# Product-key experts in another order: every query before the first batch of expert rows

## The chip, the cores and the metric

The kernel runs on one core of a Trainium2 chip. The metric is the device time of one execution in microseconds (us); the lower it is, the better.

## The reference, cut to what matters

A token sequence of 256 rows of 1024 numbers goes through two blocks: a mixer and the PEER layer, then a second mixer and a mixture of 16 dense experts. The change is in the PEER layer:

```python
q = (hf @ wq).reshape(T, PEER_HEADS, 2, PEER_QDIM // 2)          # T 256, 8 heads, 2 x 128
s = jnp.einsum('thpd,hpnd->thpn', q, subkeys)                    # 128 keys in each half
s1, i1 = lax.top_k(s[:, :, 0], 16); s2, i2 = lax.top_k(s[:, :, 1], 16)
...                                                              # 256 sums, the best 16 of them
w = jax.nn.softmax(top_s, axis=-1)                               # idx: 16 of 16384 experts
act = gelu(einsum('cd,chkd->chk', x_c, u[idx_c]))
out = einsum('chk,chkd->cd', w_c * act, v[idx_c])
```

So each token picks 8 x 16 = 128 experts, and each expert is one row of u and one row of v, 1024 float32 numbers each.

## The kernel before

The program is written as one fixed order of instructions for each engine. Four stages follow one another: `mixer1`, `peer`, `mixer2` and `experts`. The 128 partitions hold 128 tokens; there are two token tiles `tt`.

**Memory.** `Mem` hands out columns of one tile of 42440 floats per partition: `take` gives the lowest hole that is large enough, `give` returns a region. A region handed out again must wait for the readers and writers of its former content.

**Weights.** `Stream` brings the weight blocks of the first three stages in their order: 19 blocks `w_in`, 8 of `w_branch` and `w_out`, 8 blocks `wq`, then those of the second mixer, `w_in_2`. Each block is 1 MB, 2048 floats per partition, and lands in a landing region by a DMA on SP's queue. Each half of a block is then split (`split`, lines 277 and 281) into a high part (a copy on ACT) and a low part (a subtraction on DVE, or on POOL where the half's number modulo 4 is in `on_pool`). There are three landing regions and three part buffers, so the split runs three halves ahead of TensorE. When both halves of a block are split, its landing region is free: `ahead` loads the next block into it, or gives it back where `shrink` asked for that. `done` frees a part buffer and calls `ahead`, and so the next split stands in the program right behind the use of a half.

**PEER before.** Head `c` needs block `wq + c`: `features` runs 24 matmuls for each half (line 266), ACT copies the query to `qT`, and `score(c)` multiplies it by the keys (8 matmuls, two copies on ACT, line 986). `search` is a generator of DVE work for 16 pairs of token tile and head; it finds the best 16 of 128 twice (lines 971 to 974), the best 16 of 256 sums and their indices (lines 999 to 1022). `look(us)` puts about so many planned microseconds of this search on DVE; it does nothing where the scores of the next head are not there. A *slot* is one chosen expert of each of the 128 tokens of a tile; there are 256. `gather` issues for each slot an indirect DMA from POOL (line 1049) that brings 128 rows of u and v, 1 MB, into one of `RING = 10` row buffers; it may run 10 slots ahead of the finished batches, and it first puts on DVE whatever search a slot's indices still need. A `batch` handles two slots: two dot products on DVE (line 1065), Gelu on ACT (1067), a `look`, the coefficient on DVE (1069), two diagonal matrices on ACT (1073) and 4 products of 128 x 512 on TensorE, which add the v rows, scaled, into the accumulators. A row buffer is free after its slot's products.

In the loop over the 8 heads of the kernel before, the first ten gathers stand behind head 1, and one batch stands behind each of the heads 5, 6 and 7. After the loop come the other 125 batches, with `close_tile` after each token tile. When the search is over, `preload` takes regions for the second mixer out of the regions that the search leaves.

**Experts.** `Ahead` loads the experts' 192 blocks of 2 MB one after the other into regions of 4096 floats at fixed positions. `ex.take` claims those positions that are wholly free: two early in `mixer2` (line 1273), others at lines 1567 and 1680, the rest in `experts` (line 1732).

Of the kernel before, what the change touches and what calls it, by code (L numbers as in the profile page):

```python
# [14 lines left out]
OP = mybir.AluOpType  # L15
AX = mybir.AxisListType

T, D = 256, 1024
# [4 lines left out]
RING, BATCH = 10, 2  # L23
# [150 lines left out]
class Mem:  # L174
# [5 lines left out]
    def take(self, n, high=False):  # L180
        n = (n + 7) // 8 * 8
        fits = [h for h in self.holes if h[1] >= n]
        assert fits, (n, self.holes)
        h = max(fits) if high else min(fits)
        self.holes.remove(h)
        at = h[0] + h[1] - n if high else h[0]
        rest = (h[0], h[1] - n) if high else (h[0] + n, h[1] - n)
        if rest[1]:
            self.holes.append(rest)
        return at, n  # L190

    def claim(self, at, n):

        for h in self.holes:
            if h[0] <= at and at + n <= h[0] + h[1]:
                self.holes.remove(h)
                self.holes += [x for x in ((h[0], at - h[0]), (at + n, h[0] + h[1] - at - n)) if x[1]]
                return True
        return False
# [16 lines left out]
class Kernel:  # L216
# [17 lines left out]
    def sb(self, n, high=False):  # L234
        r = self.mem.take(n, high)
        return r, self.mem.at(r, n)
# [28 lines left out]
    def mm(self, out, l, r, start=True, stop=True):  # L265
        self.nc.tensor.matmul(out, l, r, start=start, stop=stop, skip_group_check=True)  # L266
# [664 lines left out]
    def peer(self):  # L931
        nc, a, mem = self.nc, self.a, self.mem
        sb, rb, drop = self.scope()
        mm = self.mm
        st, wq = self.st, self.blocks_at["wq"]
        sub = sb(2048, "keys").rearrange("p (c n) -> p c n", c=16)
        nc.scalar.dma_start(sub, a["subkeys"])
        gain = sb(D, "gain")
# [1 line left out]
        h2 = [rb(8 * T, "h2").rearrange("p (k t) -> p k t", k=8) for _ in range(2)]  # L940
        self.scaled(self.h, self.v("nffn"), *h2)
        mem.give(self.junk_region)
        st.on_pool = ()
        st.shrink(land=1)

        xn = sb(2 * D).rearrange("p (t d) -> p t d", t=2)
        for tt in range(2):
            nc.vector.scalar_tensor_tensor(xn[:, tt], self.h[:, tt], self.rs[:, tt:tt + 1], gain,
                                           op0=OP.mult, op1=OP.mult)
        drop("gain")  # L950
        self.preload_norm()
        S = [sb(2048, "scores").rearrange("p (c n) -> p c n", c=16) for _ in range(2)]
        qT = [sb(512, "keys").rearrange("p (c t) -> p c t", c=2) for _ in range(2)]

# [7 lines left out]
        idx, w, act, coef = [[sb(128) for _ in range(2)] for _ in range(4)]  # L962
        total = [sb(8) for _ in range(2)]
        diags = [sb(128) for _ in range(2 * BATCH)]
        ring = [sb(2 * D) for _ in range(RING)]

        def top16(x, v, ix):

# [9 lines left out]
        def score(h):  # L978

            b, ps = self.bank()  # L980
            for tt in range(2):
                for s in range(2):
                    mm(ps[:, (2 * tt + s) * 128:(2 * tt + s) * 128 + 128],
                       qT[h % 2][:, s, tt * 128:tt * 128 + 128], sub[:, 2 * h + s])
            for tt in range(2):
                nc.scalar.copy(S[tt][:, 2 * h:2 * h + 2],
                               ps[:, 256 * tt:256 * tt + 256].rearrange("p (c n) -> p c n", c=2))
            self.free_banks.append(b)
            self.scored = h + 1
# [38 lines left out]
        def look(us):  # L1028

            nonlocal debt  # L1030
            debt += us
            while debt > 0 and (self.searched % 8 < self.scored or self.searched >= 8):
                took = next(todo, 0)
                if not took:
                    break
                debt -= took
            debt = min(debt, 0.0)
# [5 lines left out]
        def gather():  # L1043
            nonlocal gathered
            while gathered < slots and gathered < batches * BATCH + RING:
                n, tt, k = gathered, gathered // 128, gathered % 128
                while self.searched <= n // 16:
                    next(todo)
                nc.gpsimd.indirect_dma_start(  # L1049
                    out=ring[n % RING], out_offset=None, in_=a["peer_uv"],  # L1050
                    in_offset=bass.IndirectOffsetOnAxis(ap=idx[tt].bitcast(U32)[:, k:k + 1], axis=0))
                gathered += 1

        def batch():

            nonlocal batches
            gather()
            first = batches * BATCH
            tt, k0 = divmod(first, 128)
            here = slice(k0, k0 + BATCH)  # L1060
            if k0 == 0:
                acc[2 * tt:2 * tt + 2] = [self.bank() for _ in range(2)]
            for k in range(BATCH):
                x = ring[(first + k) % RING][:, 0:D]
                nc.vector.tensor_tensor_reduce(x, x, xn[:, tt], 1.0, 0.0, OP.mult, OP.add,  # L1065
                                               act[tt][:, k0 + k:k0 + k + 1])
            nc.scalar.activation(act[tt][:, here], act[tt][:, here], AF.Gelu)  # L1067
            look(SEARCH)
            nc.vector.scalar_tensor_tensor(coef[tt][:, here], act[tt][:, here], total[tt][:, k0 // 16:k0 // 16 + 1],  # L1069
                                           w[tt][:, here], op0=OP.mult, op1=OP.mult)  # L1070
            for k in range(BATCH):
                g = diags[(first + k) % len(diags)]
                nc.scalar.activation(g, self.ident, AF.Copy, scale=coef[tt][:, k0 + k:k0 + k + 1])  # L1073
            for k in range(BATCH):
                g, x = diags[(first + k) % len(diags)], ring[(first + k) % RING]
                for n in range(2):
                    mm(acc[2 * tt + n][1], g, x[:, D + n * 512:D + n * 512 + 512], k0 + k == 0, k0 + k == 127)
            batches += 1

        for c in range(8):  # L1080
            b, ps = self.bank()
            for half in range(2):
                self.features(wq + c, h2, ps, (half,))
                look(KEYS)
            nc.scalar.copy(qT[c % 2], ps.rearrange("p (c t) -> p c t", c=2))
            self.free_banks.append(b)
            if c:
                score(c - 1)
            if c == 1:
                gather()  # L1090
            if c > 4:
                batch()
        score(7)
        drop("h2")
        while batches * BATCH < 128:
            batch()
        drop("keys")
# [1020 lines left out]
```

## Time and profile before

| what | value |
|---|---|
| median of 3 runs | 2134.71 us (2130.98 to 2134.91) |
| the profiled execution | 2133.23 us, of which the span of its instructions is 2131.4 us |
| TensorE busy | 1538.2 us, 72% |
| VectorE (DVE) busy | 844.7 us, 40% |
| ScalarE (ACT) busy | 434.8 us, 20% |
| GpSimd (POOL) busy | 372.5 us, 17% |
| moved by DMA | 734.01 MB, mean 344 GB/s |

The profile's times count from the span's start. A busy share is an average over stages with different limits, so the stages are read one by one. In the views, L1049 is line 1049 of the kernel before, PEld is TensorE's weight load, and SPq stands for a DMA issued from SP's queue. The bracket at the end of a timeline line says how long the engine had been idle and what ended that.

### The profile page before, as it was taken

What the parts mean: (1) busy time and instruction counts of PE and PEld (TensorE: products, weight loads), DVE (VectorE), ACT (ScalarE), POOL (GpSimd) and SP (SyncE); (2) the same over time, 40 slices, a digit from 0 to 9 for tenths busy, and PEclk for the clock granted to TensorE, in tenths of its full rate; (3) what the DMA queues carried; (4) which work ended last, traced back from release to release, by engine and by line L of the source; (5) the groups of instructions that cost most, each with busy time, mean ns of one, the idle gap of its engine ahead of it and who ended that gap; (6) DMA issues with size and microseconds to landing.
All of it is one profiled execution on the core that took longest, in us unless ns stands there. A gap on an engine that the chain in (4) does not pass through costs nothing.

```text
span 2131.4 us, 21789 instructions
## 1 busy us (share of the span) xinstructions
PE 1538.2 (72%) x8331; PEld 779.0 (37%) x8331; DVE 844.7 (40%) x1993; ACT 434.8 (20%) x1014; POOL 372.5 (17%) x337
## 2 busy tenths in 40 slices
PE   8999866877777777778899776565555556565656
PEld 7988843323323222227888511111111111111112
DVE  6656758999946555556852400000000000000002
ACT  4554433323312111114432300000000000000002
POOL 1000213444444333324322200000000000000000
PEclk9999978999999999999999887888888887878887
DMA  6333476999999999992123699999999999999997
GB/s 239 139 119 128 159 308 265 421 421 421 421 420 397 421 422 422 421 416 119 62 85 136 254 429 429 427 427 427 428 428 427 428 428 428 428 428 427 426 428 313
DMA packets 74986, 734.01 MB, mean 344 GB/s; under 512 B 8321, under 2 KB 9089, under 8 KB 10114
## 3 DMA queue, kind: packets, MB, share of 16 engines
q1 hardware_dynamic: 37154, 460.29, 51.9%
q0 software_dynamic: 36864, 268.45, 30.5%
q10 hardware_dynamic: 864, 3.87, 0.5%
q8 instruction: 66, 1.08, 0.2%
q14 instruction: 38, 0.31, 0.0%
HBM read 731.53 MB, written 1.05 MB: 344 GB/s over the span
## 4 chain that ended last, share of the span: by engine, by line
issue 47%; PE 19%; DVE 16%; DMA 15%; POOL 1%; ACT 1%; POOLq 0%; SPq 0%; ACTq 0%; DVEq 0%
PE bank L266 18%; DMA sbuf<-in_peer_uv_dram,sbuf 15%; DVE sbuf L1065 6%; DVE sbuf L972 2%; DVE sbuf L971 1%; POOL sbuf L1049 1%; DVE sbuf L974 1%; DVE rounded L281 1%; DVE sbuf L1232 1%; DVE sbuf L1017 0%; DVE sbuf L1018 0%; DMA sbuf<-in_wq_dram 0%; DVE sbuf L1015 0%; ACT rounded L277 0%; PE bank L800 0%
## 5 line engine op out<-in xcount | busy, mean ns | idle before, releaser
L266 PE MATMUL bank<-sbuf 128*32 128x512 f32 (+8 forms) x4032 | 927.8, 576 | 389.9 <-DMA sbuf<-in_wgu_dram 184.3
L266 PEld LDWEIGHTS bank<-sbuf 128*128 128x128 f32 (+5 forms) x3980 | 386.0, 163 | 908.4 <-issue 311.5
L1065 DVE CUSTOM_DVE_ANT_0 sbuf<-sbuf 128x1024 f32<-128x1024 f32 x256 | 308.8, 1223 | 147.8 <-DMA sbuf<-in_peer_uv_dram,sbuf 147.7
L1049 POOL DMA_INDIRECT sbuf<-in_peer_uv_dram,sbuf x256 | 268.1, 1047 | 431.3 <-PE bank L266 252.4
L266 PE MATMUL bank<-rounded 128*128 128x256 f32 (+3 forms) x2208 | 304.1, 298 | 3.6 <-DVE rounded L281 3.3
L266 PEld LDWEIGHTS bank<-rounded 128*128 128x128 f32 (+2 forms) x2208 | 285.1, 193 | 16.6 <-DVE rounded L281 3.7
L1889 DVE TENSOR_TENSOR rest<-rest,bank 128x512 f32<-128x512 f32 x16 | 11.0, 688 | 539.4 <-PE bank L266 539.4
L353 POOL TENSOR_TENSOR sbuf<-sbuf 128x1 f32<-128x1 f32 (+2 forms) x11 | 10.0, 913 | 1177.3 <-DVE sbuf L357 942.7
L266 PE MATMUL bank<-sbuf,tail 128*32 128x512 f32 (+1 forms) x960 | 131.8, 684 | 83.1 <-DMA sbuf<-in_wd_dram 78.6
L281 DVE TENSOR_TENSOR rounded<-sbuf,rounded 128x1024 fp32r<-128x1024 f32 (+2 forms) x90 | 101.7, 1146 | 97.8 <-ACT rounded L277 97.8
L277 ACT CAST rounded<-sbuf 128x1024 fp32r<-128x1024 f32 (+3 forms) x112 | 107.5, 974 | 156.6 <-PE bank L266 128.4
L1888 ACT ACTIVATE rest<-bank 128x512 f32<-128x512 f32 x16 | 9.6, 597 | 567.2 <-PE bank L266 567.2
L1881 DVE TENSOR_SCALAR sbuf<-sbuf 128x256 f32<-128x256 f32 x16 | 6.6, 414 | 292.4 <-PE bank L266 292.4
L1073 ACT ACTIVATE sbuf<-sbuf 128x128 f32<-128x128 f32 x256 | 89.1, 394 | 132.6 <-DVE sbuf L1069 127.1
L266 PE MATMUL bank<-tail,sbuf 128*32 128x512 f32 (+2 forms) x344 | 73.5, 738 | 35.1 <-DMA tail<-in_wgu_dram 23.5
L1067 ACT ACTIVATE sbuf<-sbuf 128x2 f32<-128x2 f32 x128 | 26.0, 204 | 349.3 <-DVE sbuf L1065 349.2
L266 PEld LDWEIGHTS bank<-sbuf,tail 128*32 128x32 f32 x960 | 29.2, 124 | 175.8 <-DMA sbuf<-in_wd_dram 119.0
L1909 ACT COPY tail<-bank 128x512 f32<-128x512 f32 x15 | 8.8, 585 | 292.7 <-PE bank L266 292.7
L281 POOL TENSOR_TENSOR rounded<-sbuf,rounded 128x1024 fp32r<-128x1024 f32 x22 | 53.4, 2433 | 78.4 <-ACT rounded L277 64.6
L266 PEld LDWEIGHTS bank<-tail,sbuf 128*32 128x32 f32 (+2 forms) x344 | 21.9, 164 | 90.1 <-DMA tail<-in_wgu_dram 37.2
L266 PE MATMUL bank<-rest,sbuf 128*32 128x512 f32 (+1 forms) x196 | 33.0, 775 | 22.0 <-DMA rest<-in_wgu_dram 22.0
L1069 DVE SCALAR_TENSOR_TENSOR sbuf<-sbuf 128x2 f32<-128x2 f32 x128 | 27.7, 216 | 23.8 <-ACT sbuf L1067 23.8
(274 smaller groups left out, 852.8 us busy)
## 6 DMA issues: line engine op xcount, KB each, us to landing
sbuf<-in_wgu_dram SPq DMA_DIRECT2D x104, 2048.0 KB, 39.1
sbuf<-in_wd_dram SPq DMA_DIRECT2D x48, 2048.0 KB, 39.1
sbuf<-in_w_in_dram SPq DMA_DIRECT2D x29, 1024.0 KB, 4.9
tail<-in_wgu_dram SPq DMA_DIRECT2D x12, 2048.0 KB, 39.1
rest<-in_wgu_dram SPq DMA_DIRECT2D x12, 2048.0 KB, 39.1
rest<-in_wd_dram SPq DMA_DIRECT2D x6, 2048.0 KB, 39.1
tail<-in_wd_dram SPq DMA_DIRECT2D x6, 2048.0 KB, 39.1
sbuf<-in_w_out_dram SPq DMA_DIRECT2D x8, 1024.0 KB, 4.8
```

What stands on the lines that cost most here:

```text
L266: self.nc.tensor.matmul(out, l, r, start=start, stop=stop, skip_group_check=True)
L277: nc.scalar.copy(hi.bitcast(FR), x)
L281: e.tensor_tensor(lo.bitcast(FR), x, hi, op=OP.subtract)
L971: nc.vector.max(v[:, cut], x)
L972: nc.vector.max_index(ix[:, cut].bitcast(U32), v[:, cut], x)
L974: nc.vector.match_replace(x, v[:, cut], x, -3.0e38)
L1049: nc.gpsimd.indirect_dma_start(out=ring[n % RING], out_offset=None, in_=a["peer_uv"], in_offset=bass.IndirectOffsetOnAxis(ap=idx[tt].bitca ...
L1065: nc.vector.tensor_tensor_reduce(x, x, xn[:, tt], 1.0, 0.0, OP.mult, OP.add, act[tt][:, k0 + k:k0 + k + 1])
L1067: nc.scalar.activation(act[tt][:, here], act[tt][:, here], AF.Gelu)
L1069: nc.vector.scalar_tensor_tensor(coef[tt][:, here], act[tt][:, here], total[tt][:, k0 // 16:k0 // 16 + 1], w[tt][:, here], op0=OP.mult, op ...
L1073: nc.scalar.activation(g, self.ident, AF.Copy, scale=coef[tt][:, k0 + k:k0 + k + 1])
L1232: nc.vector.scalar_tensor_tensor(y[:, i], x[:, i, j:j + 256], w[:, j:j + 1], y[:, i], op0=OP.mult, op1=OP.add)
```

## The change

All eight `wq` blocks get a landing region at once: right after the scaled activations are made, the stream grows by five regions and is told to give six back as they come free. The row buffers of the ring are no longer taken all at once at the start; each of the first ten gathers takes one if a hole of 2048 floats exists, and stops if none does. The loop over heads holds no batch any more. `score(c - 1)` stands between the two halves of head `c`, the first `gather` stands there for head 1, and the heads from 2 on end with a `gather`. The normalised token rows `xn` (`normed`) are made behind the first gathers and no longer before the loop, some low parts go to POOL until then (`on_pool = (0, 2)`), and `preload_norm` (the load of one gain vector, and a region) moves behind the loop.

```diff
+    def fits(self, n):
+        return any(h[1] >= n for h in self.holes)
...
         self.scaled(self.h, self.v("nffn"), *h2)
         mem.give(self.junk_region)
-        st.on_pool = ()
-        st.shrink(land=1)
-
+
+        st.on_pool = (0, 2)
+        st.grow(land=5)
+        st.shrink(land=6)
         xn = sb(2 * D).rearrange("p (t d) -> p t d", t=2)
-        for tt in range(2):
-            nc.vector.scalar_tensor_tensor(xn[:, tt], self.h[:, tt], self.rs[:, tt:tt + 1], gain,
-                                           op0=OP.mult, op1=OP.mult)
-        drop("gain")
-        self.preload_norm()
+
+        def normed():
+
+            for tt in range(2):
+                nc.vector.scalar_tensor_tensor(xn[:, tt], self.h[:, tt], self.rs[:, tt:tt + 1], gain,
+                                               op0=OP.mult, op1=OP.mult)
+            drop("gain")
+
...
-        ring = [sb(2 * D) for _ in range(RING)]
+        ring = []
...
                 n, tt, k = gathered, gathered // 128, gathered % 128
+                if n < RING:
+                    if not mem.fits(2 * D):
+                        break
+                    ring.append(sb(2 * D))
...
                 self.features(wq + c, h2, ps, (half,))
+                if c and half == 0:
+                    score(c - 1)
+                if c == 1 and half == 0:
+                    gather()
+                    st.on_pool = ()
+                    normed()
                 look(KEYS)
             nc.scalar.copy(qT[c % 2], ps.rearrange("p (c t) -> p c t", c=2))
             self.free_banks.append(b)
-            if c:
-                score(c - 1)
-            if c == 1:
+            if c > 1:
                 gather()
-            if c > 4:
-                batch()
         score(7)
         drop("h2")
+        self.preload_norm()
```

## Rows read from the trace of the kernel before

**Rows 1.** The page's 40 slices of the span: DMA share in tenths, GB/s.

```profile
DMA  6333476999999999992123699999999999999997
GB/s 239 139 119 128 159 308 265 421 421 421 421 420 397 421 422 422 421 416 119 62 85 136 254 429 429 427 427 427 428 428 427 428 428 428 428 428 427 426 428 313
```

**Rows 2.** Windows: length, busy time per engine, TensorE clock, DMA share, GB/s.

```profile
260.00:350.00 90.00, 56.40 (x295) 43.12 (x296) 57.60 (x167) 27.30 (x54) 18.64 (x17) 0.75 0.66 257
...
348.00:350.00 2.00, 2.00 (x5) 0.91 (x4) 2.00 (x5) 0.41 (x3) 1.61 (x1) 0.86 0.00 0
...
364.00:584.00 220.00, 174.93 (x358) 69.28 (x359) 211.60 (x662) 72.94 (x179) 98.81 (x90) 0.95 1.01 421
...
1197.00:1214.00 17.00, 8.82 (x48) 6.61 (x48) 10.97 (x30) 6.27 (x12) 4.65 (x2) 0.60 0.06 24
```

**Rows 3.** Timeline of TensorE through the query phase and the first batches.

```profile
234.83 12.40 PE L266 MATMUL bank<-rounded 128*128 128x256 f32 x96
...
261.04 5.07 PE L266 MATMUL bank<-rounded 128*128 128x256 f32 x22 [3.13 <-DVE rounded L281]
...
267.07 5.99 PE L266 MATMUL bank<-rounded 128*128 128x256 f32 x48
...
272.90 1.05 PE L266 MATMUL bank<-sbuf 128*128 128x128 f32 x8
...
292.67 6.01 PE L266 MATMUL bank<-sbuf 128*128 128x512 f32 x8 [12.07 <-ACT sbuf L1073]
...
335.46 5.99 PE L266 MATMUL bank<-sbuf 128*128 128x512 f32 x16 [9.61 <-ACT sbuf L1073]
```

**Rows 4.** Timeline of POOL: gathers 1, 10, 11, 12, 15 and 17.

```profile
260.73 1.31 POOL L1049 DMA_INDIRECT sbuf<-in_peer_uv_dram,sbuf  x1 [23.31 <-DVE sbuf L1022]
...
274.74 0.94 POOL L1049 DMA_INDIRECT sbuf<-in_peer_uv_dram,sbuf  x1 [1.53 <-DMA sbuf<-in_peer_uv_dram,sbuf]
...
296.72 0.94 POOL L1049 DMA_INDIRECT sbuf<-in_peer_uv_dram,sbuf  x1 [21.05 <-PE bank L266]
298.96 0.94 POOL L1049 DMA_INDIRECT sbuf<-in_peer_uv_dram,sbuf  x1 [1.30 <-PE bank L266]
...
339.12 1.12 POOL L1049 DMA_INDIRECT sbuf<-in_peer_uv_dram,sbuf  x1 [18.69 <-DVE sbuf L1015]
...
347.75 1.86 POOL L1049 DMA_INDIRECT sbuf<-in_peer_uv_dram,sbuf  x1 [5.98 <-DVE sbuf L1069]
```

**Rows 5.** SP's queue from 225 to 350 us.

```profile
235.08 0.33 SPq L2047 DMA_DIRECT2D sbuf<-in_wq_dram  x1
...
246.65 26.11 SPq L2047 DMA_DIRECT2D sbuf<-in_wq_dram  x4
279.13 45.59 SPq L2047 DMA_DIRECT2D sbuf<-in_w_in_dram  x3
```

**Rows 6.** Timeline of DVE and ACT: splits, the first search, a first coefficient.

```profile
237.95 2.47 DVE L948 SCALAR_TENSOR_TENSOR sbuf<-sbuf 128x1024 f32<-128x1024 f32 x2
...
245.40 1.23 DVE L281 TENSOR_TENSOR rounded<-sbuf,rounded 128x1024 fp32r<-128x1024 f32 x1 [1.67 <-ACT rounded L277]
...
249.36 0.29 DVE L971 MAX8 sbuf<-sbuf 128x8 f32<-128x128 f32 x1
...
259.71 0.15 DVE L1022 RECIPROCAL sbuf<-sbuf 128x1 f32<-128x1 f32 x1
...
281.63 1.04 ACT L277 CAST rounded<-sbuf 128x1024 fp32r<-128x1024 f32 x1 [3.79 <-DMA sbuf<-in_wq_dram]
...
291.97 0.21 DVE L1069 SCALAR_TENSOR_TENSOR sbuf<-sbuf 128x2 f32<-128x2 f32 x1
```

**Rows 7.** The page's costliest groups: the dot products of all slots.

```profile
L1065 DVE CUSTOM_DVE_ANT_0 sbuf<-sbuf 128x1024 f32<-128x1024 f32 x256 | 308.8, 1223 | 147.8 <-DMA sbuf<-in_peer_uv_dram,sbuf 147.7
```

**Rows 8.** SP's queue where the last stage begins.

```profile
1161.70 17.81 SPq L1986 DMA_DIRECT2D sbuf<-in_wgu_dram  x5
...
1191.26 0.35 SPq L1986 DMA_DIRECT2D rest<-in_wd_dram  x1
```

## The prediction

> **What bounds the kernel.** I began with the page's 40 slices [rows 1]. The DMA row has two long runs of nines: slices 7 to 17, the gathers of PEER at about 421 GB/s, and from slice 23 to the end the experts' weights at about 428. In both the transfers set the pace, whatever the 72% of TensorE says. Between the runs stand the first mixer, the start of PEER and the second mixer, where DMA is not full; time can be won or lost only there, or by moving fewer bytes, which this change doesn't do. Then the windows around the start of PEER [rows 2]: from 260 to 350 us the DMA share is 0.66, so of 90 us some 30.6 stand idle, and from 364 to 584 it is 1.01 at 421 GB/s. One gather of 1.049 MB therefore costs 1.049 / 421 = 2.49 us, and the stream is full from 350 on (0.00 in the 2 us before). Then TensorE's timeline says why the start is thin [rows 3]: a query block takes 6.0 us and its scores 1.05, but once batches stand between the blocks TensorE waits 12.07 us at 292.67 and 9.61 us at 335.46 for the diagonals of a batch (a third lies between). The queries behind the batch wait too, and so do the gathers: ten are issued from 260.73 to 274.74, then only six more before 347.75, each pair held by one batch [rows 4]. Everything behind PEER hangs on its last batch, so what PEER wins or loses reaches the end one to one, unless the second mixer's loads change.
>
> **The loads.** Before, one wq load goes out at 235.08 and four from 246.65 to 272.8, three of these among the gathers; three w_in_2 loads follow from 279.13 [rows 5]. After, the five grown regions let five more loads follow the one at 235.08 at once: wq 4 to 7 and the first w_in_2 block. Six loads are 15 us of DMA, 235 to about 251, in a stretch with nothing else to move. Between gathers remain only two w_in_2 loads. The one visible stall on such a load, 3.79 us on ACT at 281.63 [rows 6], goes.
>
> **Row buffers.** Walking through the allocator: after the five landings, xn, scores and small tiles 10768 floats are left, five row buffers; the landings of blocks 1 and 2 are back by the first half of head 1. So seven gathers go out at first, and heads 2, 3 and 4 release one each: ten, as before, but no eleventh until a batch is done.
>
> **The first gather.** A half of a block is 12.40 / 4 = 3.1 us [rows 3], so the first half of head 1 ends at 244.1 and its scores at 245.2. DVE is then in the split of 245.40, which ends at 246.6 [rows 6]; the first search, 249.36 to 259.86, 10.5 us, runs 246.6 to 257.1. The gather follows 0.9 us later, as at 260.73: 258.0, 2.7 us earlier. xn, 2.47 us on DVE, left the stretch before and now lies behind the search, to 259.6; nothing needs it before the first batch, but the split of block 3 is queued behind it. That one ends at 259.6 + 1.23 = 260.8. TensorE has used its parts up at 255.4 (245.2, plus three halves and a score), so it stalls 5.4 us, against 3.13 before, and comes back slow: before it took 0.23 us per matmul there, against 0.125 at full clock [rows 3]. I charge 2.3 us for that.
>
> **The other queries.** Block 3 begins at 260.8 and ends at 260.8 + 6.0 + 2.3 + 1.05 = 270.2, with a score in its middle. Blocks 4 to 7 take 7.05 us each: 298.4. The last copy and score: 300.5; say 301. Can DVE keep up? Per block two splits, 2.46 us, and two looks, 3 us as planned; the planner's sum for one search is 8.2 us and it took 10.5, so 3.8. That is 6.3 of 7.05. Before, block 4 took 5.99 us without a break beside such work [rows 3].
>
> **The first batch.** The split behind the last half waits for TensorE at 299, then 1.05 on ACT and 1.23 on DVE: 301.3, and the look behind it 1.9: 303.2. Two dot products at 1.223 [rows 7], a look of 2.6, the coefficient at 0.2: 308.5. From a coefficient at 291.97 [rows 6] to gather 11 at 296.72 [rows 4] it was 4.75 us at the same slow clock; so gather 11 goes out at 313.2. DMA started 2.2 us after the issue of 347.75: 315.4; I say 316, since a look ends on whole steps.
>
> **The sum.** After: at 316 the stream is full with 246 gathers to go. Before: at 350, with 240 to go. The six are 6 x 2.49 = 14.9 us. Gain 350 - 316 - 14.9 = 19 us. The bytes as a cross-check: before, 0.66 x 90 = 59.4 us of DMA work between 260 and 350, in which 16 gathers (39.8), three wq and three w_in_2 loads (15) explain 55; after, from 258 to 316 ten gathers and two loads, 30 us, and 28 idle. So most of the idle time stays, now in one piece, and the gain is chiefly that 10 us of loads leave it, with 2.7 us of an earlier start and 2.6 us less idle time: 15. The other 4 us is DMA work before that the loads don't explain. I take 19, by the first way; 15 is inside the range.
>
> The Trainium skill ("DMA: Bandwidth & Descriptors", section Specifications) puts the HBM limit of one core at about 358 GB/s; by it a gather would be an estimated 2.93 us and the gain 350 - 316 - 17.6 = 16. This trace holds 421 GB/s over 220 us [rows 2], and the measurement decides.
>
> **Behind PEER.** Other regions are held now, and I followed them to the experts. The positions at 17864 and 13768 are covered by zs and junk until the second mixer ends, so at line 1680 three are claimed where five were, and the other two at line 1732. Two of the five loads from 1161.70 on therefore move beside the one at 1191.26 [rows 8]: 3 x 4.98 us (2.097 MB at 421), done at about 1206. From 1197 to 1214 DMA stands nearly idle (0.06) [rows 2], which covers the two; without that cover they cost 9.8 us. The two earlier claims stay. Taken as nothing. preload_norm's load (0.5 MB) and its region, and one low part moved to POOL in a stretch where DVE waits, are nothing as well: neither is waited for before the first batch.
>
> The profiled execution took 2133.2 us; 2133.2 - 19 = 2114. The median of the runs is 1.5 us above it: 2116.
>
> **Rivals.** *DVE becomes the bound until the search is over.* Between 364 and 584 DVE is busy 211.6 of 220 us with DMA full [rows 2], so it has 4% to spare. Were a batch 5.2 us where DMA wants 4.97, the 52 batches or so that carry the remaining 12.8 searches (12.8 x 8.2 / 2) would lose 12 us: gain 7, 2128. Against it: before, DMA is full beside just that work. 0.12. *The expert loads come late* (the cover fails because a claimed region waits for junk's last reader, behind 1191): 9.8 lost, gain 9, 2126. 0.08. *Queries are slower than TensorE:* gather 11 waits for all of them, so each us is lost once. The gain is gone when they end 19 us later, at 320, that is when blocks 3 to 7 take 10.9 us each. Looks could do that if DVE needed 10.9 us per block in place of 6.3; if all looks ran at twice their plan, 2.46 + 6 = 8.5 us per block, the queries end 7 us later and the gain is 12. For a loss of 8 us (2143) blocks of 12.5 us are needed. Between 316 and 324 there is no difference to see. Slower 0.07, no difference 0.05. The loads not coming first (a grown region still in use by the first mixer) would go the same way: they are wanted at 255 at the earliest, 20 us after the issue, and only beyond that cost anything.
>
> **Numbers.** My forecast, with 0.68, spans gains of 11 to 27 us: at the upper end block 3 neither stalls nor runs slow (5.4 + 2.3 less), at the lower all looks at twice their plan. Range for 8 in 10: 2106 to 2128, which takes in the first two rivals at their middle. A difference under 0.2%, 4.3 us, can't be told from none here. Faster 0.68 + 0.12 + 0.08 = 0.88, same 0.05, slower 0.07.
>
> **What would show it.** wq loads all issued by 237; the first gather near 258, seven in one go; TensorE with one stall near 255 and no wait for diagonals before 305; score 7 near 300; no gather between about 285 and 313; DMA full from 316 to the end of PEER, which comes 19 us earlier; nine expert blocks loaded before the first is used, still. Wrong if the last query ends past 310, if DMA falls under 0.97 between 320 and 560, or if the experts' stream begins late.

## The result, and the profile after

The changed kernel takes **2110.17 us** (median of 4 runs, 2109.42 to 2112.19) against 2133.12 us before (4 runs, 2130.98 to 2134.91): ratio **0.9894**, 95% interval 0.9877 to 0.9911. It is faster by 23 us; 19 were forecast (2116 us), and the measured time lies inside the range given. The profiled execution of after has a span of 2107.7 us, the one of before 2131.4: 23.7 us less, and these are what the traces must account for. The file grew by a few lines: L269 is the matmul helper, L280 and L284 the split, L955 `normed()`, L993 the copy of the scores, L1014 the search's Exp, L1060 the gather, L1076 a dot product, L1080 a batch's coefficient, L1084 its diagonals, L1102 the copy of a finished query.

The page's slices answer to [rows 1]: the run of nines that is PEER begins a slice earlier (slices are 52.7 us now), and the thin slice ahead of it moved no more than 250 GB/s.

```profile
DMA  6333669999999999973123899999999999999997
GB/s 241 136 111 135 229 250 416 422 421 421 421 422 395 421 421 421 422 325 140 41 105 115 340 428 428 427 428 428 428 428 428 427 428 428 428 427 428 428 428 313
```

The windows of after show the new shape of the start (columns as in [rows 2]).

```profile
240.00:258.00 18.00, 13.93 (x107) 13.72 (x106) 12.65 (x43) 6.46 (x12) 2.40 (x1) 0.87 0.67 278
258.00:285.00 27.00, 25.65 (x208) 25.44 (x207) 24.76 (x69) 11.43 (x20) 13.19 (x10) 0.96 0.91 363
285.00:314.00 29.00, 19.77 (x116) 15.34 (x116) 26.34 (x78) 13.62 (x26) 2.87 (x2) 0.82 0.36 125
314.00:340.00 26.00, 20.33 (x45) 7.85 (x44) 25.00 (x84) 7.74 (x20) 13.25 (x13) 1.00 0.99 407
340.00:560.00 220.00, 168.46 (x350) 66.55 (x351) 205.49 (x639) 71.62 (x175) 93.68 (x87) 0.95 1.01 421
1183.00:1197.00 14.00, 13.74 (x93) 8.57 (x91) 4.42 (x12) 3.32 (x7) 0.00 (x0) 0.80 0.46 170
1197.00:1220.00 23.00, 20.63 (x176) 7.45 (x174) 4.17 (x10) 2.94 (x4) 0.00 (x0) 1.00 1.00 426
```

Loads and first gathers fill 258 to 285 (share 0.91), then comes one hole of 29 us at 0.36, and from 314 on the stream is full, where before it was from 350 on [rows 2]. TensorE's timeline, which answers to [rows 3], says what fills the hole: queries with no batch between them, and no batch until 306.76.

```profile
245.27 5.99 PE L269 MATMUL bank<-rounded 128*128 128x256 f32 x48
255.34 2.08 PE L269 MATMUL bank<-sbuf 128*128 128x128 f32 x8 [4.07 <-ACT sbuf L1102]
257.07 7.33 PE L269 MATMUL bank<-rounded 128*128 128x256 f32 x48
...
265.05 5.99 PE L269 MATMUL bank<-rounded 128*128 128x256 f32 x48
272.40 1.16 PE L269 MATMUL bank<-sbuf 128*128 128x128 f32 x8 [1.35 <-ACT sbuf L1102]
...
293.26 3.11 PE L269 MATMUL bank<-rounded 128*128 128x256 f32 x24
297.92 1.16 PE L269 MATMUL bank<-sbuf 128*128 128x128 f32 x8 [1.55 <-ACT sbuf L1102]
306.76 8.51 PE L269 MATMUL bank<-sbuf 128*128 128x512 f32 x14 [7.68 <-ACT sbuf L1084]
```

POOL's timeline (to be read beside [rows 4]) has gathers 1, 2, 10, 11 and the last one; below it stands the last one of before.

```profile
258.18 1.37 POOL L1060 DMA_INDIRECT sbuf<-in_peer_uv_dram,sbuf  x1 [12.96 <-ACT sbuf L993]
259.85 2.92 POOL L1060 DMA_INDIRECT sbuf<-in_peer_uv_dram,sbuf  x1 [0.30 <-issue]
...
275.84 0.93 POOL L1060 DMA_INDIRECT sbuf<-in_peer_uv_dram,sbuf  x1 [2.97 <-DVE rounded L284]
310.81 1.84 POOL L1060 DMA_INDIRECT sbuf<-in_peer_uv_dram,sbuf  x1 [34.04 <-DVE sbuf L1080]
...
921.54 0.94 POOL L1060 DMA_INDIRECT sbuf<-in_peer_uv_dram,sbuf  x1 [0.78 <-DVE sbuf L1076]
```

```profile
943.91 0.94 POOL L1049 DMA_INDIRECT sbuf<-in_peer_uv_dram,sbuf  x1 [0.78 <-DVE sbuf L1065]
```

So 22.4 of the 23.7 us are won by the last gather (943.91 - 921.54). SP's queue, which answers to [rows 5] and [rows 8], shows the loads: all of wq by 237.9 and the first w_in block right behind it, and at the experts three blocks early, the others behind.

```profile
210.48 27.39 SPq L2061 DMA_DIRECT2D sbuf<-in_wq_dram  x8
237.91 57.33 SPq L2061 DMA_DIRECT2D sbuf<-in_w_in_dram  x3
...
1147.93 8.46 SPq L2000 DMA_DIRECT2D sbuf<-in_wgu_dram  x3
...
1168.85 28.64 SPq L2000 DMA_DIRECT2D sbuf<-in_wd_dram  x4
```

### The profile page after: what moved, and what is told of

It reads as the page before. It is cut to its first block, busy times and chain, and to the rows that moved or that the text cites. A ratio compares the mean times of both kernels' runs of the same rounds, so it can differ in the third digit from the quotient of the medians.

```text
span 2107.7 us, 21793 instructions
## 1 busy us (share of the span) xinstructions
PE 1543.1 (73%) x8331; PEld 776.8 (37%) x8331; DVE 843.6 (40%) x1992; ACT 433.1 (21%) x1012; POOL 375.1 (18%) x338
## 3 DMA queue, kind: packets, MB, share of 16 engines
HBM read 731.53 MB, written 1.05 MB: 348 GB/s over the span
## 4 chain that ended last, share of the span: by engine, by line
issue 46%; PE 20%; DMA 19%; DVE 13%; POOL 1%; ACT 1%; POOLq 0%; SPq 0%; ACTq 0%; DVEq 0%
DMA sbuf<-in_peer_uv_dram,sbuf 19%; PE bank L269 19%; DVE sbuf L1076 5%; DVE sbuf L979 1%; DVE sbuf L978 1%; DVE rounded L284 1%; DVE sbuf L981 1%; DVE sbuf L1246 1%; POOL sbuf L1060 0%; PE bank L803 0%; DVE sbuf L1024 0%; PE bank L1441 0%; DVE sbuf L1025 0%; DVE sbuf L1022 0%; POOL sbuf L356 0%
## 5 line engine op out<-in xcount | busy, mean ns | idle before, releaser
L269 PE MATMUL bank<-sbuf 128*32 128x512 f32 (+8 forms) x4016 | 921.2, 575 | 368.3 <-DMA sbuf<-in_wgu_dram 175.8
L269 PEld LDWEIGHTS bank<-sbuf 128*128 128x128 f32 (+5 forms) x3964 | 384.2, 163 | 883.5 <-issue 309.8
L1076 DVE CUSTOM_DVE_ANT_0 sbuf<-sbuf 128x1024 f32<-128x1024 f32 x256 | 309.6, 1223 | 151.0 <-DMA sbuf<-in_peer_uv_dram,sbuf 150.7
L1060 POOL DMA_INDIRECT sbuf<-in_peer_uv_dram,sbuf x256 | 268.6, 1049 | 400.6 <-PE bank L269 214.3
L269 PE MATMUL bank<-rounded 128*128 128x256 f32 (+3 forms) x2208 | 302.6, 297 | 0.5 <-DVE rounded L284 0.2
L269 PEld LDWEIGHTS bank<-rounded 128*128 128x128 f32 (+2 forms) x2208 | 283.5, 192 | 13.0 <-DVE rounded L389 2.1
L356 POOL TENSOR_TENSOR sbuf<-sbuf 128x1 f32<-128x1 f32 (+2 forms) x11 | 10.1, 914 | 1175.9 <-DVE sbuf L360 942.4
L269 PE MATMUL bank<-sbuf,tail 128*32 128x512 f32 (+1 forms) x1024 | 141.5, 695 | 75.1 <-DMA sbuf<-in_wd_dram 67.7
L280 ACT CAST rounded<-sbuf 128x1024 fp32r<-128x1024 f32 (+3 forms) x112 | 107.6, 974 | 139.4 <-PE bank L269 112.3
L284 DVE TENSOR_TENSOR rounded<-sbuf,rounded 128x1024 fp32r<-128x1024 f32 (+3 forms) x89 | 100.6, 1145 | 76.1 <-ACT rounded L280 76.0
L1084 ACT ACTIVATE sbuf<-sbuf 128x128 f32<-128x128 f32 x256 | 89.1, 394 | 130.4 <-DVE sbuf L1080 129.4
L269 PE MATMUL bank<-tail,sbuf 128*32 128x512 f32 (+2 forms) x344 | 73.9, 735 | 35.3 <-DMA tail<-in_wgu_dram 23.8
L269 PEld LDWEIGHTS bank<-sbuf,tail 128*32 128x32 f32 x1024 | 33.0, 130 | 169.9 <-DMA sbuf<-in_wd_dram 107.5
L284 POOL TENSOR_TENSOR rounded<-sbuf,rounded 128x1024 fp32r<-128x1024 f32 x23 | 55.4, 2416 | 83.8 <-ACT rounded L280 55.1
L269 PEld LDWEIGHTS bank<-tail,sbuf 128*32 128x32 f32 (+2 forms) x344 | 22.1, 164 | 92.6 <-DMA tail<-in_wgu_dram 35.6
L269 PE MATMUL bank<-rest,sbuf 128*32 128x512 f32 (+1 forms) x212 | 35.4, 770 | 26.4 <-DMA rest<-in_wgu_dram 26.4
L1080 DVE SCALAR_TENSOR_TENSOR sbuf<-sbuf 128x2 f32<-128x2 f32 x128 | 27.7, 217 | 20.6 <-ACT sbuf L1078 20.6
```

Source lines behind the costliest of these rows:

```text
L280: nc.scalar.copy(hi.bitcast(FR), x)
L284: e.tensor_tensor(lo.bitcast(FR), x, hi, op=OP.subtract)
L1060: nc.gpsimd.indirect_dma_start(out=ring[n % RING], out_offset=None, in_=a["peer_uv"], in_offset=bass.IndirectOffsetOnAxis(ap=idx[tt].bitca ...
```

## The experiments

The change does three things at once: the batches leave the query loop (A), the query weights are loaded first (B), and the first gather goes out earlier (C). The theories are named after them: A says that the gain comes from the batches, so that time is lost or won one to one with the time of gather 11, the first that needs a finished batch; B and C say the loads or the first gather. The ratios are to the kernel before, run on the same chip. Gather 11 marks the start of the full stream only where no batch stands among the queries: in the kernel before it went out earlier, at 296.72, but only five more followed it before the stream was full [rows 4].

**The order alone, on the kernel before.**

```diff
-            if c > 4:
-                batch()
```

> The kernel before without the batches behind heads 5, 6 and 7, and nothing else of the change. Theory A (the gain comes from taking the batches out of the query loop, so that the eleventh gather no longer waits behind stalled queries): the last score falls from 341 us to 285 to 305, the eleventh gather is issued between 300 and 316 (in the changed kernel 310.8), and the time is 2108 to 2119, most of the 23 us. Theory B (the gain comes from loading the query weights ahead of the gathers): the loads still stand behind ten gathers, the queries wait for them, and no more than 6 us are won: 2127 to 2133. Theory C (the gain is the earlier first gather): nothing, 2131 to 2135.

Measured: 2114.49 us (2110.61 to 2116.70), ratio 0.9903 [0.9880, 0.9926]. Two deleted lines bring nearly all of it. Its TensorE timeline, and below it POOL's, with L1085 the copy of a query and L1073 the diagonals in the lines of before:

```profile
302.46 2.07 PE L266 MATMUL bank<-sbuf 128*128 128x128 f32 x8 [6.55 <-ACT sbuf L1085]
309.38 9.90 PE L266 MATMUL bank<-sbuf 128*128 128x512 f32 x16 [4.85 <-ACT sbuf L1073]
```

```profile
313.44 0.94 POOL L1049 DMA_INDIRECT sbuf<-in_peer_uv_dram,sbuf  x1 [37.53 <-DVE sbuf L1000]
```

Gather 11 goes out 2.6 us after that of the changed kernel, and the median is 4.3 us above it; the intervals of the two ratios overlap.

**The loads first alone: the changed kernel with its batches back in the query loop**, behind a head's gathers.

```diff
+            if c > 4:
+                batch()
```

> The changed kernel with one batch put back behind each of the heads 5, 6 and 7; the loads stay first and the first gather early. Theory A: TensorE again waits 8 to 12 us for the diagonals of each of these batches, the last score falls past 325, and at most 13 us remain of the gain (10 us of loads out of the gathers' stretch and 2.7 of the earlier start): 2120 to 2131. Theory B: the gain stays at 18 us or more, under 2115. Theory C: about 3 us, 2130.

Measured: 2132.56 us (2129.08 to 2135.74), ratio 0.9996 [0.9985, 1.0008]. Nothing is left of the gain. TensorE's timeline shows the three waits for diagonals again, as in [rows 3]:

```profile
292.54 6.20 PE L269 MATMUL bank<-sbuf 128*128 128x512 f32 x8 [9.52 <-ACT sbuf L1084]
...
316.37 6.23 PE L269 MATMUL bank<-sbuf 128*128 128x512 f32 x8 [11.00 <-ACT sbuf L1084]
...
337.38 6.86 PE L269 MATMUL bank<-sbuf 128*128 128x512 f32 x16 [8.14 <-ACT sbuf L1084]
```

This kernel has the early first gather too (258.13), so with the loads C brings nothing either. Theory A had left up to 13 us to loads and gather, 2120 to 2131, and was too generous: the median lies above that range. The window from 260 to 350 shows why, beside the same window of before [rows 2]: the query loads are out of it, but its DMA share only falls, from 0.66 to 0.58, and the gathers come no earlier (gather 11 at 296.59).

```profile
260.00:350.00 90.00, 57.92 (x332) 44.36 (x331) 60.34 (x182) 29.15 (x53) 18.40 (x17) 0.81 0.58 219
```

Both runs together: A holds, though its share for the loads does not, and B falls. The early loads by themselves bring nothing, and most of the gain comes without them.

**The first gather late: the changed kernel with scores and first gathers at the end of a head's loop.**

```diff
-                if c and half == 0:
-                    score(c - 1)
-                if c == 1 and half == 0:
-                    gather()
-                    st.on_pool = ()
-                    normed()
...
-            if c > 1:
+            if c:
+                score(c - 1)
+            if c:
                 gather()
+            if c == 1:
+                st.on_pool = ()
+                normed()
```

> The changed kernel with each score, and the first gather, at the end of a head's loop, where the kernel before had them. Theory A: the first gather is 3 us later, but the ten gathers still land long before the eleventh can be issued, so the time stays within 2 us of the changed kernel: 2108 to 2112. Theory C: the 2.7 us are lost in full or more, 2113 and above.

Measured: 2106.63 us (2102.12 to 2108.05), ratio 0.9874 [0.9855, 0.9894]: below what any theory said. The first gather is 2.1 us later (260.27) and C falls; but the last score starts at 296.36, 1.6 us earlier, and gather 11 is 3.5 us earlier:

```profile
307.35 0.94 POOL L1060 DMA_INDIRECT sbuf<-in_peer_uv_dram,sbuf  x1 [30.60 <-PE bank L269]
```

**The first batch 10 us later: the changed kernel with 10 us of planned search ahead of the batches.**

```diff
         score(7)
+        look(10.0)
```

> The changed kernel with 10 planned units of the search (about 12.8 us of DVE work as the first search showed) put on DVE between the last query and the first batch; the work is only moved forward. Theory A (each us by which the eleventh gather is late is lost once): the eleventh gather near 322, the time 10 to 13 us above the changed kernel, 2120 to 2123. The rival that DVE is the bound until the search is over: search done early is not to be done later, so the time is within 3 us of the changed kernel, 2107 to 2113.

Measured: 2122.11 us (2121.19 to 2122.59), ratio 0.9945 [0.9927, 0.9964]. On POOL's timeline gather 11 is 11.8 us later than in the changed kernel, and the median 11.9 (by the ratios 10.9):

```profile
322.62 1.09 POOL L1060 DMA_INDIRECT sbuf<-in_peer_uv_dram,sbuf  x1 [46.55 <-PE bank L269]
```

The rival, that search done early need not be done later, had at most 3 us, and falls. The four kernels that have no batch among the queries and ten gathers ahead of them keep one order: gather 11 at 307.35, 310.81, 313.44 and 322.62 us, medians 2106.6, 2110.2, 2114.5 and 2122.1. From end to end that is 15.5 us of time for 15.3 us of lateness. The medians are of several executions and the gathers of one; in the profiled executions themselves the last dot product of PEER ends at 937.3, 941.3, 945.4 and 952.0, 14.7 us from end to end. One to one holds over the whole distance; single steps are off by up to 2.6 us.

**An eleventh row buffer**, for the idle stretch: its region is freed by giving back PEER's small buffers before the last landing is grown.

```diff
-RING, BATCH = 10, 2
+RING, BATCH = 11, 2
...
+        drop()
         st.grow(land=1)
         self.dump("h2", self.h)
-        drop()
```

> The changed kernel with a ring of 11 row buffers (the eleventh in the landing of block 6; the second mixer's extra landing is taken after the ring is given back, which moves some later regions). Theory A: DMA stands nearly idle from about 285 to 313 us, so one more gather fits there, and 2.5 us are won against the changed kernel: 2106 to 2109. The rival that the stretch before the first batch is not what holds the stream: no difference, 2109 to 2112.

Measured: 2107.12 us (2103.57 to 2111.09), ratio 0.9879 [0.9857, 0.9901]. The eleventh gather does go out in the hole, at 281.89. The median is 3 us lower, but the intervals overlap: whether it counts can't be told from the times. The traces say where it went. Below are the last dot product of PEER and the last w_in load of the second mixer, with eleven row buffers and then in the changed kernel:

```profile
937.26 1.23 DVE L1076 CUSTOM_DVE_ANT_0 sbuf<-sbuf 128x1024 f32<-128x1024 f32 x1 [1.23 <-DMA sbuf<-in_peer_uv_dram,sbuf]
...
1092.17 0.33 SPq L2061 DMA_DIRECT2D sbuf<-in_w_in_dram  x1
```

```profile
940.07 1.23 DVE L1076 CUSTOM_DVE_ANT_0 sbuf<-sbuf 128x1024 f32<-128x1024 f32 x1 [1.22 <-DMA sbuf<-in_peer_uv_dram,sbuf]
...
1090.71 0.33 SPq L2061 DMA_DIRECT2D sbuf<-in_w_in_dram  x1
```

PEER ends 2.8 us earlier, near the 2.5 of theory A, but the second mixer's load goes out 1.5 us later: what PEER wins is lost before 1092. The regions behind PEER were moved for this variant; that this is the cause is not shown.

**Batches among the queries, in two parts.** If the wait for the diagonals is all that is wrong with a batch among the queries, then a batch whose products are put off until later should fill the hole for nothing. `batch()` is split into `front()` (dots, coefficient, diagonals) and `back()` (products).

```diff
+                if fronted > batches and half == 0:
+                    back()
+                    gather()
                 look(KEYS)
...
+            if c > 2:
+                front(0.0)
         score(7)
+        back()
```

> The changed kernel with batches in the query loop again, but cut in two: the dot products, Gelu, coefficient and diagonals behind heads 3 to 7 (without a look), and the products on TensorE behind the first half of the next head, so that TensorE need not wait for the diagonals. Theory A: what cost the 23 us was the wait, not the batches' own work. The loop gets about 15 us longer (four times 3.7 us of products), but eight to ten gathers are issued in it, the idle stretch of DMA from 285 to 313 fills, and the time is 2090 to 2100. The rival that any batch among the queries costs what it brings (DVE has no room for 2.5 us more per head): 2108 or above.

Measured: 2127.41 us (2124.82 to 2129.29), ratio 0.9974 [0.9963, 0.9986]: 17 us worse than the changed kernel, and far from the 2090 to 2100 of theory A. TensorE's timeline, and a window of it right behind the wait:

```profile
282.67 6.31 PE L269 MATMUL bank<-rounded 128*128 128x256 f32 x48
288.81 1.06 PE L269 MATMUL bank<-sbuf 128*128 128x128 f32 x8
293.68 6.41 PE L269 MATMUL bank<-sbuf 128*128 128x512 f32 x8 [3.81 <-ACT sbuf L1085]
```

```profile
293.70:297.70 4.00, 4.00 (x5) 1.83 (x6) 2.67 (x9) 1.70 (x4) 0.00 (x0) 0.50 0.00 0
```

A head takes 17 us (288.81 to 305.69 from score to score): the wait of 3.0 to 4.1 us is still there, four times. In the 4 us behind the first three the granted clock is 0.50, and their products take 6.2 to 6.4 us. The front stood on VectorE behind a split and a look: the split of the next weights (start 287.14) comes after a cast on ACT (286.06) that runs when TensorE leaves the half before, the look follows, and the dots begin at 290.35. TensorE left the half before at about 285.8 (282.67 and half of 6.31), so from there to the first product it is 7.9 us, and TensorE has only the next half and a score, 4.2 us, to cover them. Two variants kept the wait. The same with eleven row buffers:

> The kernel with the batches in two parts, with a ring of 11. Theory A: with gathers issued all through the query loop DMA has no idle stretch left for an eleventh row to fill, so no more than 2.5 us are won against the batches in two parts with ten rows.

Measured: 2126.15 us (2124.07 to 2129.85), ratio 0.9976 [0.9965, 0.9988], 1.3 us below ten row buffers, as expected. And the same with scores and first gathers at the loop's end:

> The kernel with the batches in two parts, with the scores and the first gather at the end of a head's loop. With batches at the end of the loop (the changed kernel) this place was worth about 4 us, because no half of block 2 waited for the first search on ACT. Theory A: with gathers all through the loop the later first gather costs 2 to 3 us, and the shorter loop wins 3 to 4: within 3 us of the batches in two parts.

Measured: 2122.88 us (2117.28 to 2125.61), ratio 0.9947 [0.9933, 0.9962]. That is 4.5 us below the first of the three, more than the 3 expected, but again with waits of 3.0 to 4.1 us for the diagonals, of which this is one:

```profile
290.31 6.55 PE L269 MATMUL bank<-sbuf 128*128 128x512 f32 x8 [3.02 <-ACT sbuf L1085]
```

So far either reading stood: the wait is the price, or any batch among queries costs what it brings.

**The front half a head earlier.** One move tells them apart: `front()` goes behind a head's first half, ahead of the look, with the rest as in the last variant. A second half, a score and a first half then lie between front and products, and ahead of them the products of the batch before.

```diff
                 if fronted > batches and half == 0:
                     back()
                     gather()
+                if c > 2 and half == 0:
+                    front(0.0)
                 look(KEYS)
...
-            if c > 2:
-                front(0.0)
         score(7)
```

> The batch in two parts once more, with the scores at the end of a head's loop, but its front (dots, coefficient, diagonals) put behind the first half of heads 3 to 7 instead of behind the second, its products behind the first half of the next head. In the run with the front behind the second half the diagonals came some 10 us after that block's end while TensorE had about 4 us of work left, so it waited 3.0 to 4.1 us each time. Now a second half, a score and a first half, some 7 to 8 us of TensorE work, lie between. Theory that the wait for the diagonals is the whole price: the waits fall to about 1 us each, a head takes 11 to 13 us instead of 17, gathers run on from about 275 us, and the time is 2090 to 2104 us. Rival, any batch among the queries costs as much as it brings since all of it goes through VectorE and ScalarE, which then hold up the split of the next weights: 2112 us or more, with the waits moved from the diagonals to the split or to the copy of the query.

Measured: **2100.27 us** (2097.93 to 2103.07), ratio 0.9835 [0.9815, 0.9855]. TensorE's timeline, and three windows:

```profile
279.73 1.05 PE L269 MATMUL bank<-sbuf 128*128 128x128 f32 x8
280.53 3.12 PE L269 MATMUL bank<-rounded 128*128 128x256 f32 x24
283.71 3.70 PE L269 MATMUL bank<-sbuf 128*128 128x512 f32 x8
286.85 3.43 PE L269 MATMUL bank<-rounded 128*128 128x256 f32 x24
```

```profile
283.70:287.30 3.60, 3.59 (x9) 1.67 (x10) 1.94 (x7) 3.57 (x8) 1.87 (x2) 1.00 1.01 426
...
285.00:314.00 29.00, 26.32 (x166) 20.99 (x164) 25.01 (x65) 15.00 (x32) 6.54 (x6) 1.00 1.01 407
314.00:340.00 26.00, 20.57 (x45) 9.51 (x46) 24.14 (x72) 10.67 (x25) 9.13 (x8) 0.87 0.80 293
```

The wait is gone at heads 5 to 7 (at head 4, the first, it is 1.66 us), the clock stays at 1.00, a head takes 10.2 us (283.71 to 293.89) with its batch in it, and the hole of 29 us is full: DMA share 1.01 where the changed kernel had 0.36. That is what the theory of the wait said, and the rival falls: the one move is worth 22.6 us against the variant before it (2122.88; by the ratios, since the chips differ, 24). The wait and the slow clock behind it went together, so the run does not price them apart. Eighteen gathers are out by 308 instead of ten. A part is given back behind it, where the share is 0.80 from 314 to 340.

**Two small gains put together**, the late first gather and the eleventh row buffer, and **the changed kernel again**, on the chip of the last run:

> Two things that looked good singly, put together: scores and first gathers at the end of a head's loop (2106.6 us alone) and an eleventh row buffer (2107.1 us alone), no batch in the query loop. If both are real and add up, 2102 to 2106 us. If each only looked good within its interval: 2107 to 2111 us, like the change itself.

> The changed kernel itself, on the same chip as the two others, so that a few us between it and them can be told: 2108 to 2113 us, as before.

Measured: 2108.68 us (2105.12 to 2110.74), ratio 0.9870 [0.9850, 0.9890], and 2110.36 us (2107.37 to 2112.52), ratio 0.9881 [0.9863, 0.9899]. The two can't be told apart, so the small gains don't add up to anything that was shown; in this trace too the second mixer's last w_in load comes late behind an early end of PEER (1089.90, where the late first gather alone has 1084.50). The gain of the late first gather rests on one run of 4 executions and the agreement of its trace with the order above. The version with the earlier front is 10.1 us below the change on the same chip, with intervals that don't touch: it is the best of all, and beats both kernels.

## Why the prediction was right

*What bounds the kernel.* As put: what the start of PEER wins reaches the end one to one. The delayed batch shows it, 11.8 us of lateness for 10.9 to 11.9 us of time.

*The loads.* As put, all wq loads are issued by 237.9. But I let them carry the cross-check ("the gain is chiefly that 10 us of loads leave it"), and that reading fell: loads first alone gave 0.9996, the order alone 0.9903. Loads that shared the start of PEER with gathers cost nothing there, because DMA had idle time beside them: taken out, they left a share of 0.58 in place of 0.66. The 15 us of that way were too few; its 28 us of idle DMA were too many as well, for 258 to 316 has about 21 (0.09 x 27 + 0.64 x 29 + 0.13 x 2, with a share of 0.87 from 314 to 316).

*Row buffers and first gather.* Ten gathers and then none until a batch, as put; the first at 258.18, where 258.0 was worked out. Nine go out without a break, the last of these at 271.94, so the trace neither shows nor denies the seven in one go. "2.7 us of an earlier start" brought nothing by itself: the run with a late first gather was not slower.

*The stall.* I had TensorE stall 5.4 us at the split of block 3, at 255.4, and charged 2.3 us for the low clock behind it. That stall did not come. TensorE had already waited 4.07 us half a block earlier, ahead of score 1, and run slow behind that: 2.4 us more for the score and the two halves after it (2.08 + 7.33 for 1.05 + 5.99). Score 1 waits for the copy of its query, and that copy stands in ACT's queue behind the search's Exp, which waits for VectorE; the rows of ACT:

```profile
253.47 0.31 ACT L1014 ACTIVATE sbuf<-sbuf 128x16 f32<-128x16 f32 x1 [7.26 <-DVE sbuf L1013]
...
254.71 0.57 ACT L1102 COPY sbuf<-bank 128x512 f32<-128x512 f32 x1
```

I had named VectorE's queue and not ACT's. The same wait comes back with 1.35 us at 272.40 and 1.55 us at 297.92. The split that I had named ends where I put it, at about 260.8 (the first of two from 259.61), but TensorE comes to block 3 only at 261.4, and with the granted clock back at 1.00, since the slow stretch lay before it:

```profile
259.61 2.36 DVE L284 TENSOR_TENSOR rounded<-sbuf,rounded 128x1024 fp32r<-128x1024 f32 x2
```

```profile
255.30:260.00 4.70, 4.67 (x22) 4.67 (x23) 4.53 (x10) 1.58 (x3) 1.52 (x2) 0.50 0.00 0
```

Block 3 could not have begun before that split, so 260.8 was a sound bound; but what TensorE waited for was something else, and that it came out within 0.6 us of the bound is in part luck. A stall at that split does show in the run with the late first gather, where the score stands behind the second half:

```profile
262.96 4.40 PE L269 MATMUL bank<-rounded 128*128 128x256 f32 x22 [5.17 <-DVE rounded L284]
```

*The other queries.* Block 3 ended at 268.1 and not at 270.2; from there to the end of block 7's products (296.4) it took 28.3 us, where four blocks of 7.05 make 28.2. VectorE kept up, and the rival of slow queries did not come.

*The first batch.* The dots begin at 300.86 (I had 303.2), the coefficient is there at 306.07 (308.5), gather 11 goes out 4.74 us after it (I took 4.75 from before). The batch itself is as put, 10 us from its dots to gather 11; it only begins earlier. **The mis-sized term** is thus the 2.3 us for the low clock behind the stall of block 3: block 3 ran at full clock and ended 2.1 us before the forecast, and gather 11 went out at 310.81 and not 313.2. DMA was full from 314.4 in effect (shares of 0.87 and 0.93 up to 318), not from 316.

*The sum.* 350 - 314.4 - 14.9 = 20.7 us. The last gather is 22.4 us earlier: 1.7 us lie somewhere in the 600 us of the full stream, 0.3% of it, and 1.3 us behind PEER. I have no row that explains either; the four executions of the changed kernel lie 2.8 us apart. With 23.7 in place of 19, the sum of the prediction gives 2111 us.

*Behind PEER.* As put: three blocks are claimed early, the others wait, the gap from 1183 to 1197 (share 0.46) takes them, and from 1197 on the stream is full. The rival of late expert loads did not come. Nor did that of VectorE as the bound: it is busy 205.49 of 220 us from 340 to 560, with DMA at 1.01.

## What to carry to other kernels

When an in-order engine must wait in the middle of a loop for work that another engine does for it, count the work that lies between the request and the use. In the two-part run TensorE had 4.2 us of work to cover a chain of 7.9 us, and the time was 17 us above the plain order; with the request half a pass earlier it had 10.2 us, the products of the batch before included, no wait was left at heads 5 to 7, and the time was 10 us below it. Moving such work out of the loop altogether is the safe part of the gain, about two thirds of what the best version has over the kernel before (ratios 0.9894 and 0.9835). Count from what the request itself waits for: here the dots stand on VectorE behind a split that TensorE's last half releases. And a change that does several things at once is best tried with each undone: here two deleted lines did most of the work, and the rearranged loads alone did none of it.

## What the runs showed of the hardware

TensorE's clock made a short wait dear. In the two-part run the granted clock was 0.50, the 1.2 GHz level, in the 4 us behind a wait of 3.81 us, and eight products took 6.41 us; in the run without the wait it was 1.00, 2.4 GHz, and they took 3.70. Behind the changed kernel's waits of 1.35 and 1.55 us a score took 1.16 us, against 2.08 behind the one of 4.07. The Trainium skill ("TensorE: Matmul & The Clock Gate", section HAM oscillation — how this bites in real kernels) describes a loop in which every pass waits and falls back to the slow clock again; the trace of the two-part run agrees, with four such waits, one to a head.

The issue of one gather on POOL mostly takes 0.94 us, but the second took 2.92 us in the changed kernel and 4.05 us where the first gather was late. In both it lies beside VectorE's splits with two inputs, of which two stand there in the one (259.61 to 261.97) and three in the other:

```profile
261.69 3.49 DVE L284 TENSOR_TENSOR rounded<-sbuf,rounded 128x1024 fp32r<-128x1024 f32 x3
...
261.94 4.05 POOL L1060 DMA_INDIRECT sbuf<-in_peer_uv_dram,sbuf  x1 [0.30 <-issue]
```

Both issues end 0.8 us behind the last split (262.77 and 265.99). The whole trace of the changed kernel shows the same: of its 256 gathers 59 took longer than 0.97 us to issue, and 58 of these end 0.81 us behind the end of a VectorE instruction with two inputs (a split, a dot product, a step of the search) that ran beside them, while those issued beside the search's one-input MAX8 took 0.94 (three issues beside a two-input instruction were not held up). The Trainium skill ("SBUF — State Buffer", section SBUF: two separate sides) says that VectorE with two inputs in SBUF and a GpSimd operation that reads SBUF lock each other out of a shared pair of ports for the whole instruction. That would fit, and no run here separates it from other causes; the one exception is the first gather, which took 1.37 us and ends 1.05 us behind the instruction of `normed()` beside it.
